# The last down product's low weight parts made by ScalarE and accumulating DMAs, its sums moved to other PSUM banks

## The chip, the cores and the metric

The kernel runs on one core of a Trainium2 chip. The metric is the device time of one execution in microseconds (us); lower is better. The number given for a kernel is the median of several executions; the profile is of one further execution.

## The reference

It is one decoder layer over 512 tokens of width 1024: a token mixer (convolution and retention branches), then a gated MLP, each followed by a residual and a LayerNorm. Only the end of the MLP matters here:

```
def channel_mixer(h, w_up, ffn_dw_w, ffn_dw_b, w_down):
    u = jnp.einsum("bsd,df->bsf", h, w_up)
    u = causal_depthwise_conv(u, ffn_dw_w, ffn_dw_b)
    val, gate = jnp.split(u, 2, axis=-1)
    return jnp.einsum("bsf,fd->bsd", val * jax.nn.silu(gate), w_down)
...
        f = channel_mixer(h, w_up[l], ffn_dw_w[l], ffn_dw_b[l], w_down[l])
        x = layer_norm(DEEPNORM_ALPHA * x + gate2 * f, ln2_g[l], ln2_b[l])
```

The einsum with w_down is (512 x 2816) by (2816 x 1024); its result is gated, added to the residual and normalised row by row.

## The kernel before

Every float32 factor is split into a high part (rounded to float32r) and a low part (the factor less its high part), and a product is made of three matmuls: high by high, low by high, high by low. In `sub_mm` these are the three `mm` lines, L1113, L1114 (both read the weight's high part) and L1115 (reads its low part).

The down product is not done as one product. Rows, columns and the sum over 2816 are each halved, and seven products of 256 x 512 outputs over 1408 (11 blocks k of 128) take the place of eight, with sums of weight blocks (T1 to T4) in place of some blocks. T1 to T4 lie in DRAM; GpSimd made them long before, with copying and accumulating DMAs (L634, L639; an accumulating DMA adds what it reads to what lies at its destination). The seventh product uses T4 = 11 blocks of 128 x 512.

Each product of the loop over n has two PSUM tiles, t = 0 and 1 (128 rows each). R1, R2 and R3 are pairs of PSUM banks that hold the sums ca, c5 and so on. Product 6 (n = 5) writes R3; the seventh, after the loop, goes on adding to R3: t = 0 over 512 columns, t = 1 over two halves of 256 columns, one after the other, so that the first half's end can be worked on while the second is multiplied. `gated` multiplies a sum by the gate row and adds it to or takes it from the residual row x; `finish` takes the LayerNorm statistics (bn_stats, bn_aggr), asks GpSimd for rstd, runs two pairs of scalar_tensor_tensor (L912, L913) on VectorE and stores two halves of 256 KB from SP's queue.

Weights come through `Stream`. For the first six products SP loads 1 MB pieces into one of two buffers (`stage`), ScalarE writes the high part `wh`, VectorE the low part `wl` = stage - wh. For the seventh, `get_into` does the same in pieces of 512 columns into pages of their own (`wph`, `wpl`), so that all 11 blocks can be there at once: 11 ScalarE instructions (L161) and 11 VectorE subtractions (L162). T4 comes in three loads, stage90 and stage91 (four blocks, 1024 KB each) and stage92 (three blocks, 768 KB); stage91's load waits for the last reader of stage89, stage92's for the last reader of stage90. The program order on each engine is set by a scheduler at build time that works with priorities; each engine then runs its rows strictly in that order.

Of the kernel before, what the change touches and what calls it, by code (L numbers as in the profile page):

```python
# [9 lines left out]
F32 = mybir.dt.float32  # L10
F32R = mybir.dt.float32r
I32 = mybir.dt.int32
AF = mybir.ActivationFunctionType
ALU = mybir.AluOpType
# [13 lines left out]
NK = NF // 2  # L28
# [74 lines left out]
class Stream:  # L103
# [44 lines left out]
            self.ready.append((wh, wl))  # L148
            self.load(i + 1)

    def get_into(self, alloc):

        nc = self.nc
        assert self.used == len(self.ready)
        i, o, w = self.subs[self.used]
        self.load(i)
        hs, ls = [], []
        for c in range(0, w, 512):
            h, l = alloc("wph", F32R), alloc("wpl", F32R)
            src = self.stage[i][:, o + c:o + c + 512]  # L160
            nc.scalar.activation(h, src, AF.Copy)  # L161
            nc.vector.tensor_tensor(l, src, h.bitcast(F32), ALU.subtract)  # L162
            hs.append(h)
            ls.append(l)
        self.load(i + 1)
        self.ready.append(None)
        self.used += 1
        return hs, ls
# [10 lines left out]
def block_kernel(ctx: ExitStack, tc: tile.TileContext, a, out):  # L179
    nc = tc.nc  # L180
    act = nc.scalar.activation
    tt = nc.vector.tensor_tensor
# [4 lines left out]
    @contextmanager  # L187
    def later(n):
        p = tc.cur_priority
        tc.cur_priority = p + n  # L190
        yield
        tc.cur_priority = p
# [8 lines left out]
    def pg(name, dt=F32, shape=(P, S)):  # L201
        uid[0] += 1
        return pgp.tile(list(shape), dt, tag="pg", bufs=NPG, name=f"{name}_{uid[0]}")

    def ps(name, shape=(P, S)):
        uid[0] += 1
        return psp.tile(list(shape), F32, tag="ps", bufs=8, name=f"{name}_{uid[0]}")
# [88 lines left out]
    st = Stream(nc, base, entries, 2)  # L296
# [20 lines left out]
    o = VEC["bada"][0]  # L317
    nc.sync.dma_start(vec[:, o:], a["vec"][:, o:])
    xh = []
    for s in range(NS):  # L320
        r = [pg("x"), pg("x")]
# [22 lines left out]
    o = VEC["bada"][0]  # L344
# [143 lines left out]
    def rotary(i, pq, e, nm):  # L488
        sw = ht("sw", [P, S])
        b = vc("bin", e)  # L490
        act(sw[0:64], pq[64:128], AF.Identity, bias=b[64:128])
        act(sw[64:128], pq[0:64], AF.Identity, bias=b[0:64])
        f = ht("t1", [P, S], bufs=2)
        stt(f, pq, b, ctab, ALU.add, ALU.mult)
        tt(sw, sw, stab, ALU.mult)
        tt(f, f, sw, ALU.add)
        xh_ = ht(nm + "h", [P, S], F32R, bufs=2 if nm == "q" else 1)
        xl_ = ht(nm + "l", [P, S], F32R, bufs=2 if nm == "q" else 1)
        split_to(xh_, xl_, f)
        return f, xh_, xl_  # L500
# [144 lines left out]
    for i in range(NH):  # L645
        if i == 0:
# [3 lines left out]
            k = rotary(i, pk, E_K + i, "k")  # L650
            v = values(i, st.get(), st.get())
        else:
# [14 lines left out]
            k = rotary(i, pk, E_K + i, "k")  # L667
# [14 lines left out]
    def gate_unit(e, j, alloc):  # L682
        p_ = ps("gate")
        fm_unit(p_, st.get(), hs)
        t = alloc("th")
        act(t, p_, AF.Tanh, bias=bhalf[:, e + j:e + j + 1], scale=0.5)
        return t
# [94 lines left out]
    def gate_row(c0, alloc, dalloc):  # L782
        rows, parts = [], []
        for half in range(2):
            dg = dalloc("dgr")
            dgh, dgl = xdg("dgh"), xdg("dgl")
            tt(dg.rearrange("p (k q) -> p k q", q=P), ident[:, None, :].broadcast_to([P, 4, P]),
               mods[:, c0 + 4 * half:c0 + 4 * half + 4].unsqueeze(2).broadcast_to([P, 4, P]), ALU.mult)
            split_to(dgh, dgl, dg)
            parts.append((dgh, dgl))  # L790
        yield None
        for half in range(2):
            dgh, dgl = parts[half]
            p_ = ps("row")
            mm(p_, onesr, dgh, start=True, stop=False)
            mm(p_, onesr, dgl, start=False, stop=True)
            r = alloc("grow")
            act(r, p_, AF.Copy)
            rows.append(r)
        yield rows  # L800
# [15 lines left out]
    for j in range(ND):  # L816
        p_ = ps("yb")
        for half in range(2):
            wh, wl = st.get()
            for kk in range(8):  # L820
                k = 8 * half + kk
# [28 lines left out]
    xs = []  # L850
# [10 lines left out]
    for j in range(ND):  # L861
        t = gate_unit(16, j, lg)
# [10 lines left out]
        x, y = pg("mh", F32R), pg("ml", F32R)  # L873
# [35 lines left out]
    def norm_rows(x, chunks, grow, brow, done=None):  # L909
        rs, nmu = layer_stats(chunks, mean_only=True)  # L910
        for j in range(2):
            stt(x[j], x[j], nmu, grow[j], ALU.subtract, ALU.mult)  # L912
            stt(x[j], x[j], rs, brow[j], ALU.mult, ALU.add)  # L913
            if done is not None:
                done(j)
# [3 lines left out]
    for half in range(2):  # L919
        wh, wl = st.get()  # L920
        for s in range(NS):
            sl = slice(s * P, (s + 1) * P)
            d = pt0[s // 2][:, s % 2]
            for kk in range(4):
                k = 4 * half + kk
                w = slice(kk * 256, (kk + 1) * 256)
                mh, ml = m_hl[k]
                f = k == 0 and s % 2 == 0
# [139 lines left out]
    for j in range(3, NF):  # L1068
        if j == 8:
            g2 = gate_row(40, cig, cig)  # L1070
# [11 lines left out]
    ca, c5, cb_, cc_ = [[dt0[:, 2 * n + t] for t in range(2)] for n in range(4)]  # L1082
    lnr = []
    for n, name in enumerate(("ln2_g", "ln2_b")):
        r = [dt1[:, 2 * n + h] for h in range(2)]
# [4 lines left out]
    g2 = rows["gate2"]  # L1090

    def finish(s, cols=(slice(0, 512),)):
        norm_rows(xs[s], [xs[s][1]] + [xs[s][0][:, c] for c in cols], ln2g, ln2b,
                  lambda j: nc.sync.dma_start(out[s * P:(s + 1) * P, j * 512:(j + 1) * 512], xs[s][j]))

    R1, R2, R3 = [[ps(f"d{n}") for _ in range(2)] for n in range(3)]


    def make(n, i):

        x, y = F[2 * i], F[2 * i + 1]
        if n == 2:
            o = split_op(i, x[:, 0:256])
            tt(x[:, 0:256], y[:, 0:256], x[:, 0:256], ALU.subtract)
            return o
        src = {3: x[:, 0:256], 4: y[:, 0:256], 5: x[:, 256:], 6: y[:, 256:]}[n]
        return split_op(i, src, neg=(n == 6))

    def sub_mm(R, o, w, c, t, d, start, stop):
        wh, wl = w  # L1110
        sl = slice(t * P, (t + 1) * P)
        r = R[t][:, d]
        mm(r, o[:, 0, sl], wh[:, c], start=start, stop=False, skip_group_check=True)  # L1113
        mm(r, o[:, 1, sl], wh[:, c], start=False, stop=False, skip_group_check=True)  # L1114
        mm(r, o[:, 0, sl], wl[:, c], start=False, stop=stop, skip_group_check=True)  # L1115

    ALL = slice(0, 512)

    def gated(x, src, g, op, dst=None):

        dst = src if dst is None else dst
        tt(dst, src, g, ALU.mult)
        tt(x, x, dst, op)

    operands = {0: ops1, 1: ops5}
    last = []
# [6 lines left out]
    for n, R in enumerate((R1, R2, R2, R2, R1, R3)):  # L1133
        new = n in (0, 1, 5)
        ops = operands.pop(n)
        made = []
        for q in range(6):
            w = st.get(ahead=min(2, 5 - q) if n == 5 else None)
            if n == 5 and q == 5:
                for _ in range(6):  # L1140
                    last += zip(*st.get_into(last_page))
            for kk in range(2 if q < 5 else 1):
                k = 2 * q + kk
                for t in range(2):
                    sub_mm(R, ops[k], w, slice(kk * 512, (kk + 1) * 512), t, ALL, new and k == 0, k == NK - 1)
                if n:
                    made.append(make(n + 1, k))
        if made:
            operands[n + 1] = made
        if n == 0:  # L1150
            for t in range(2):
                act(ca[t], R1[t], AF.Copy)
        elif n == 1:
            for t in range(2):
                act(c5[t], R2[t], AF.Copy)
        elif n == 2:
            for t in range(2):
                tt(cb_[t], R2[t], ca[t], ALU.subtract)  # L1158
            with later(60):
                for t in range(2):  # L1160
                    tt(ca[t], ca[t], g2[1], ALU.mult)
                    stt(xs[t][1], xs[t][1], ALPHA, ca[t], ALU.mult, ALU.subtract)
            with later(120):
                for t in range(2):
                    tt(c5[t], c5[t], cb_[t], ALU.subtract)
                    resid(xs[2 + t][0], c5[t], g2[0])
                    resid(xs[2 + t][1], cb_[t], g2[1])
        elif n == 3:
            for t in range(2):
                gated(xs[t][1], R2[t], g2[1], ALU.add)  # L1170
        elif n == 4:
            with later(30):
                for t in range(2):
                    resid(xs[t][0], R1[t], g2[0])
                    finish(t)
        else:
            for t in range(2):
                gated(xs[2 + t][1], R3[t], g2[1], ALU.add, cc_[t])

    ops = operands.pop(6)  # L1180
    for t, cols in ((0, (ALL,)), (1, (slice(0, 256), slice(256, 512)))):
        for c in cols:
            for k in range(NK):
                sub_mm(R3, ops[k], last[k], c, t, c, False, k == NK - 1)
            gated(xs[2 + t][0][:, c], R3[t][:, c], g2[0][:, c], ALU.subtract)
        finish(2 + t, cols)


# [95 lines left out]
```

## Time and profile before

| | |
|---|---|
| median of 3 executions | 1067.66 us (1067.57 to 1071.11) |
| profiled execution, its own time | 1068.0 us |
| its span, first to last instruction | 1066.2 us |
| TensorE (PE) busy | 1038.7 us, 97% of the span |
| VectorE (DVE) busy | 840.4 us, 79% |
| ScalarE (ACT) busy | 488.9 us, 46% |
| GpSimd (POOL) busy | 64.3 us, 6% |
| mean granted TensorE clock | 0.998 |

The time of an execution is 1.8 us more than its span. TensorE has work nearly all the time, so a change counts where it makes TensorE wait, or in what still has to run after its last matmul.

### The profile page before, as it was taken

To read this page: it belongs to the slowest core of one execution; us is meant where nothing else is said; L and a number is where in the kernel's file an instruction comes from. 1 tells how busy PE (TensorE), PEld (TensorE's weight loads), DVE (VectorE), ACT (ScalarE), POOL (GpSimd) and SP (SyncE) were. 2 spreads that over 40 slices of the span, in tenths; PEclk is the share of its full clock that TensorE was granted. 3 is DMA by queue.
4 is the path that set the end of the run, shared out by engine and by line. 5 is a ranking of instruction groups with operands and counts; after the bars stand their busy time and mean duration, and the time that the engine had idled before them with its cause. 6 is when DMAs were issued, how large, how long until landed. Compare 5 with 4: busy or idle time off the path is not lost. (4 is left out here: it accounts for less than half of the span.)

```text
span 1066.2 us, 13773 instructions
## 1 busy us (share of the span) xinstructions
PE 1038.7 (97%) x5351; PEld 883.0 (83%) x5351; DVE 840.4 (79%) x1372; ACT 488.9 (46%) x728; POOL 64.3 (6%) x77
## 2 busy tenths in 40 slices
PE   4999999999999999999999999999999999999996
PEld 2788898989898989888888888889888888887775
DVE  7989999979797979489894445777566666669897
ACT  5754444353534453461353333264444444457631
POOL 2000202020211110000000000110000000000000
PEclk9999999999999999999999999999999999999999
DMA  8822648182829392368663246112323222255562
GB/s 317 306 95 88 210 129 232 62 225 80 249 87 223 114 275 80 119 218 289 216 244 108 90 157 231 47 40 80 119 80 98 100 89 110 79 172 179 181 212 96
DMA packets 46596, 163.24 MB, mean 153 GB/s; under 512 B 4033, under 2 KB 17601, under 8 KB 35266
## 3 DMA queue, kind: packets, MB, share of 16 engines
q1 hardware_dynamic: 33922, 139.29, 37.0%
q0 software_dynamic: 12608, 23.07, 9.8%
q8 instruction: 42, 0.69, 0.2%
q14 instruction: 24, 0.20, 0.1%
HBM read 160.25 MB, written 25.17 MB: 174 GB/s over the span
## 5 line engine op out<-in xcount | busy, mean ns | idle before, releaser
L146 ACT ACTIVATE wh<-stage 128x1024 fp32r<-128x1024 f32 x177 | 185.0, 1045 | 275.0 <-PE up L467 56.1
L147 DVE TENSOR_TENSOR wl<-stage,wh 128x1024 fp32r<-128x1024 f32 x177 | 213.1, 1204 | 123.1 <-PE up L469 57.4
L485 DVE SCALAR_TENSOR_TENSOR conv<-ci,vec,conv 128x512 f32<-128x512 f32 x240 | 179.3, 748 | 2.3
L466 PE MATMUL up<-h,wh 128*128 128x512 f32 x304 | 118.3, 389 | 0.0
L467 PE MATMUL up<-h,wh 128*128 128x512 f32 x304 | 118.3, 389 | 0.0
L469 PE MATMUL up<-h,wl 128*128 128x512 f32 x304 | 75.1, 389 | 0.0
L515 PE MATMUL v<-wl,h 128*128 128x256 f32 x256 | 72.5, 283 | 0.4 <-DVE wl L147 0.4
L514 PE MATMUL v<-wh,h 128*128 128x256 f32 x256 | 72.4, 283 | 0.0
L513 PE MATMUL v<-wh,h 128*128 128x256 f32 x256 | 72.4, 283 | 0.0
L467 PEld LDWEIGHTS up<-h,wh 128*128 128x128 f32 x304 | 57.1, 188 | 11.8
L469 PEld LDWEIGHTS up<-h,wl 128*128 128x128 f32 x304 | 57.1, 188 | 11.9
L466 PEld LDWEIGHTS up<-h,wh 128*128 128x128 f32 x304 | 57.0, 188 | 11.8
L1113 PE MATMUL d<-wh,op 128*128 128x512 f32 x132 | 52.1, 396 | 0.2 <-DVE dtmp L1158 0.2
L1114 PE MATMUL d<-wh,op 128*128 128x512 f32 x132 | 52.1, 394 | 0.0
L1115 PE MATMUL d<-wl,op 128*128 128x512 f32 x132 | 51.9, 395 | 0.0
L823 PE MATMUL yb<-rh,wh 128*128 128x512 f32 x128 | 51.0, 398 | 0.0
L824 PE MATMUL yb<-rl,wh 128*128 128x512 f32 x128 | 50.5, 395 | 0.0
L825 PE MATMUL yb<-rh,wl 128*128 128x512 f32 x128 | 50.5, 395 | 0.0
L466 PE MATMUL gate<-h,wh 128*128 128x512 f32 x128 | 50.2, 392 | 0.0
L467 PE MATMUL gate<-h,wh 128*128 128x512 f32 x128 | 49.9, 390 | 0.0
L515 PEld LDWEIGHTS v<-wl,h 128*128 128x128 f32 x256 | 49.1, 192 | 0.6 <-DVE wl L147 0.6
L513 PEld LDWEIGHTS v<-wh,h 128*128 128x128 f32 x256 | 49.1, 192 | 0.0
(306 smaller groups left out, 2474.5 us busy)
## 6 DMA issues: line engine op xcount, KB each, us to landing
stage<-in_wstep SPq DMA_DIRECT2D x29, 1024.0 KB, 5.3
stage<-in_wup SPq DMA_DIRECT2D x22, 1024.0 KB, 4.8
wb<-in_wada SPq DMA_DIRECT2D x32, 512.0 KB, 5.4
stage<-in_wret SPq DMA_DIRECT2D x8, 1024.0 KB, 5.8
stage<-in_wga SPq DMA_DIRECT2D x8, 1024.0 KB, 4.8
stage<-T SPq DMA_DIRECT2D x8, 1024.0 KB, 4.9
wa<-in_wada SPq DMA_DIRECT2D x14, 512.0 KB, 7.1
T<-in_wdn POOLq DMA_DIRECT2D x4, 1024.0 KB, 13.6
```

Source lines behind the costliest of these rows:

```text
L146: nc.scalar.activation(wh[:, :w], src, AF.Copy)
L147: nc.vector.tensor_tensor(wl[:, :w], src, wh[:, :w].bitcast(F32), ALU.subtract)
L466: mm(dst, wh[:, k * P:(k + 1) * P], hs[k][0], start=(k == 0), stop=False)
L467: mm(dst, wh[:, k * P:(k + 1) * P], hs[k][1], start=False, stop=False)
L469: mm(dst, wl[:, k * P:(k + 1) * P], hs[k][0], start=False, stop=(k == n - 1))
L485: stt(o, ci[:, t:t + S], vc("cw", i * CK + t), o, ALU.mult, ALU.add)
L513: mm(d, h_h[:, k, sl], wh[:, r], start=(k == 0), stop=False)
L514: mm(d, h_l[:, k, sl], wh[:, r], start=False, stop=False)
L515: mm(d, h_h[:, k, sl], wl[:, r], start=False, stop=(k == ND - 1))
L1113: mm(r, o[:, 0, sl], wh[:, c], start=start, stop=False, skip_group_check=True)
L1114: mm(r, o[:, 1, sl], wh[:, c], start=False, stop=False, skip_group_check=True)
L1115: mm(r, o[:, 0, sl], wl[:, c], start=False, stop=stop, skip_group_check=True)
```

## The change

For the seventh product alone, `get_into` gets `adds=True`. In place of VectorE's subtraction, ScalarE writes the low part's page as minus the high part, and a DMA issued by GpSimd adds the weight block to it out of DRAM (T4), 256 KB each: 11 VectorE instructions go, 11 ScalarE instructions and 11 accumulating DMAs come. Each low part has to wait for its ScalarE instruction and then for its DMA.

The seventh product no longer adds to R3. It starts fresh sums: t = 0 in R1[0], t = 1 in R2[0] (columns 0 to 255) and R2[1] (256 to 511). R3, the sum of product 6, is put into x by four further VectorE instructions (a multiplication and a subtraction for each t) ahead of it.

```diff
-    def get_into(self, alloc):
+    def get_into(self, alloc, adds=False):
...
             nc.scalar.activation(h, src, AF.Copy)
-            nc.vector.tensor_tensor(l, src, h.bitcast(F32), ALU.subtract)
+            if adds:
+                nc.scalar.activation(l, h.bitcast(F32), AF.Copy, scale=-1.0)
+                for f, x in self.entries[i][0]:
+                    nc.gpsimd.dma_start(l[:, f], x[:, (o + c) // 512], accum_op=ALU.add)
+            else:
+                nc.vector.tensor_tensor(l, src, h.bitcast(F32), ALU.subtract)
...
-                    last += zip(*st.get_into(last_page))
+                    last += zip(*st.get_into(last_page, adds=True))
...
+    for t in range(2):
+        tt(c5[t], R3[t], g2[0], ALU.mult)
+        tt(xs[2 + t][0], xs[2 + t][0], c5[t], ALU.subtract)
     ops = operands.pop(6)
-    for t, cols in ((0, (ALL,)), (1, (slice(0, 256), slice(256, 512)))):
-        for c in cols:
+    H = (slice(0, 256), slice(256, 512))
+    for t, parts in ((0, [(R1[0], ALL, ALL)]), (1, [(R2[h], H[0], H[h]) for h in range(2)])):
+        for r, d, c in parts:
             for k in range(NK):
-                sub_mm(R3, ops[k], last[k], c, t, c, False, k == NK - 1)
-            gated(xs[2 + t][0][:, c], R3[t][:, c], g2[0][:, c], ALU.subtract)
-        finish(2 + t, cols)
+                sub_mm({t: r}, ops[k], last[k], c, t, d, k == 0, k == NK - 1)
+            gated(xs[2 + t][0][:, c], r[:, d], g2[0][:, c], ALU.subtract)
+        finish(2 + t, [c for _, _, c in parts])
```

In the rows below, d2_838 and d2_839 are R3[0] and R3[1], d0_834 is R1[0], d1_836 and d1_837 are R2[0] and R2[1]; wph_896 to wph_916 are the high parts of blocks 0 to 10 (even numbers), wpl_897 to wpl_917 the low parts. What stands in brackets is what a row waits for: an engine, or a DMA (DMASW: one issued by GpSimd, DMAHW: one issued by SP). In the rows of the changed kernel the line numbers are 6 higher than before.

TensorE at the start of the seventh product, before:

```order
L1113 MATMUL d2_838_8294<-wph_896_9090,op_886_8992 128x512 [waits DVE_49,Activation_49]
L1114 MATMUL d2_838_8294<-wph_896_9090,op_886_8992 128x512
L1115 MATMUL d2_838_8294<-wpl_897_9091,op_886_8992 128x512
L1113 MATMUL d2_838_8294<-wph_898_9094,op_887_9001 128x512 [waits Activation_49]
L1114 MATMUL d2_838_8294<-wph_898_9094,op_887_9001 128x512
L1115 MATMUL d2_838_8294<-wpl_899_9095,op_887_9001 128x512
```

and with the change:

```order
L1119 MATMUL d0_834_8290<-wph_896_9090,op_886_8992 128x512 [waits Activation_49]
L1120 MATMUL d0_834_8290<-wph_896_9090,op_886_8992 128x512
L1121 MATMUL d0_834_8290<-wpl_897_9091,op_886_8992 128x512 [waits DMASW4_49]
L1119 MATMUL d0_834_8290<-wph_898_9095,op_887_9001 128x512 [waits Activation_49]
L1120 MATMUL d0_834_8290<-wph_898_9095,op_887_9001 128x512
L1121 MATMUL d0_834_8290<-wpl_899_9096,op_887_9001 128x512 [waits DMASW5_49]
L1119 MATMUL d0_834_8290<-wph_900_9102,op_888_9014 128x512 [waits Activation_49]
L1120 MATMUL d0_834_8290<-wph_900_9102,op_888_9014 128x512
```

The first row no longer waits for VectorE; each row that reads a low part now waits for a DMA of GpSimd.

TensorE at the end of the seventh product, from the row that waits for block 9's low part (wpl_915) on, with the change:

```order
L1121 MATMUL d0_834_8290<-wpl_915_9140,op_895_9087 128x512 [waits DMASW6_49]
L1119 MATMUL d0_834_8290<-wph_916_9144,op_918_9155 128x512
L1120 MATMUL d0_834_8290<-wph_916_9144,op_918_9155 128x512 [waits DVE_49]
L1121 MATMUL d0_834_8290<-wpl_917_9145,op_918_9155 128x512 [waits DMASW4_49]
L1119 MATMUL d1_836_8292<-wph_914_9139,op_895_9087 128x256
L1120 MATMUL d1_836_8292<-wph_914_9139,op_895_9087 128x256
L1121 MATMUL d1_836_8292<-wpl_915_9140,op_895_9087 128x256
L1119 MATMUL d1_836_8292<-wph_916_9144,op_918_9155 128x256
L1120 MATMUL d1_836_8292<-wph_916_9144,op_918_9155 128x256
L1121 MATMUL d1_836_8292<-wpl_917_9145,op_918_9155 128x256
L1120 MATMUL d1_837_8293<-wph_908_9124,op_892_9060 128x256
L1121 MATMUL d1_837_8293<-wpl_909_9125,op_892_9060 128x256
```

Behind the wait for wpl_915 stand three more rows of d0, six of d1_836 and fourteen of d1_837, of which the first two are shown. Before, 33 rows of 256 columns, the whole second half of t = 1, stood last.

VectorE at the end, before, from the multiplication of the first half of t = 1 on (mv_78, rstd_80, xr_628 and xr_629 belong to t = 0, mv_81, xr_635 and xr_636 to t = 1):

```order
L1122 TENSOR_TENSOR d2_839_8295<-d2_839_8295,grow_758_7297 128x256 [waits PE_49]
L243 BN_AGGR mv_78_9189<-bnst_918_9186 128x2 [waits DVE_49]
L1123 TENSOR_TENSOR xr_635_5884<-xr_635_5884,d2_839_8295 128x256 [waits DVE_49]
L245 TENSOR_SCALAR ve_79_9191<-mv_78_9189 128x1 [waits DVE_49]
L912 SCALAR_TENSOR_TENSOR xr_628_5812<-xr_628_5812,mv_78_9189,drow_8285 128x512
L912 SCALAR_TENSOR_TENSOR xr_629_5814<-xr_629_5814,mv_78_9189,drow_8285 128x512
L913 SCALAR_TENSOR_TENSOR xr_628_5812<-xr_628_5812,rstd_80_9193,drow_8285 128x512 [waits DVE_49,Pool_49]
L913 SCALAR_TENSOR_TENSOR xr_629_5814<-xr_629_5814,rstd_80_9193,drow_8285 128x512 [waits DVE_49]
L241 BN_STATS bnst_919_9271<-xr_635_5884 128x6
L1122 TENSOR_TENSOR d2_839_8295<-d2_839_8295,grow_758_7297 128x256 [waits PE_49]
L1123 TENSOR_TENSOR xr_635_5884<-xr_635_5884,d2_839_8295 128x256 [waits DVE_49]
```

and with the change, from the same step on:

```order
L1129 TENSOR_TENSOR xr_635_5884<-xr_635_5884,d1_836_8292 128x256 [waits DVE_49]
L247 BN_STATS bnst_918_9201<-xr_628_5812 128x6 [waits DVE_49]
L1128 TENSOR_TENSOR d1_837_8293<-d1_837_8293,grow_758_7297 128x256 [waits PE_49]
L249 BN_AGGR mv_78_9204<-bnst_918_9201 128x2 [waits DVE_49]
L247 BN_STATS bnst_919_9286<-xr_635_5884 128x6
L251 TENSOR_SCALAR ve_79_9206<-mv_78_9204 128x1 [waits DVE_49]
L918 SCALAR_TENSOR_TENSOR xr_628_5812<-xr_628_5812,mv_78_9204,drow_8285 128x512
L918 SCALAR_TENSOR_TENSOR xr_629_5814<-xr_629_5814,mv_78_9204,drow_8285 128x512
L919 SCALAR_TENSOR_TENSOR xr_628_5812<-xr_628_5812,rstd_80_9208,drow_8285 128x512 [waits DVE_49,Pool_49]
L919 SCALAR_TENSOR_TENSOR xr_629_5814<-xr_629_5814,rstd_80_9208,drow_8285 128x512 [waits DVE_49]
L1129 TENSOR_TENSOR xr_635_5884<-xr_635_5884,d1_837_8293 128x256
L247 BN_STATS bnst_919_9286<-xr_635_5884 128x6 [waits DVE_49]
```

The multiplication of the second half of t = 1 stood behind the whole LayerNorm of t = 0 (mv_78 to the two rstd_80 rows); now it stands ahead of it.

## Rows read from the trace of the kernel before

**Rows 1.** Windows: us, busy of PE, PEld, DVE, ACT, POOL, PEclk, DMA share, GB/s

```profile
1039.50:1041.20 1.70, 0.04 (x1) 0.01 (x1) 1.70 (x5) 0.33 (x1) 0.00 (x0) 1.00 0.96 378
1041.20:1058.40 17.20, 15.99 (x99) 14.23 (x99) 14.31 (x27) 3.54 (x7) 0.89 (x1) 1.00 0.24 82
```

**Rows 2.** Timeline of PE: start us, us, instruction, [idle before, releaser]

```profile
1039.14 0.40 PE L1115 MATMUL d<-wl,op 128*128 128x512 f32 x1
1041.22 0.47 PE L1113 MATMUL d<-wph,op 128*128 128x512 f32 x1 [1.68 <-DVE dtmp L1122]
...
1058.05 0.28 PE L1115 MATMUL d<-wpl,op 128*128 128x256 f32 x1
```

**Rows 3.** Chain that ended last: start us, us, what, in the seventh product

```profile
1049.93 0.23 PE d L1114
...
1057.97 0.12 PE d L1113
```

**Rows 4.** Timeline of DVE while PE waited

```profile
1039.78 0.69 DVE L162 TENSOR_TENSOR wpl<-stage,wph 128x512 fp32r<-128x512 f32 x1
1040.38 0.69 DVE L1122 TENSOR_TENSOR dtmp<-d,grow 128x512 f32<-128x512 f32 x1
```

**Rows 5.** Timeline of ACT: the high parts of T4's first two loads

```profile
1033.96 2.20 ACT L161 ACTIVATE wph<-stage 128x512 fp32r<-128x512 f32 x4 [0.96 <-DMA stage<-T]
1040.87 2.19 ACT L161 ACTIVATE wph<-stage 128x512 fp32r<-128x512 f32 x4 [4.71 <-DMA stage<-T]
```

**Rows 6.** Timeline of SP, and stage91's DMA: KB, us to landing

```profile
1035.84 0.33 SPq L130 DMA_DIRECT2D stage<-T  x1
1038.29 0.99 SPq L1094 DMA_DIRECT2D out<-xr  x2
...
stage<-T SPq DMA_DIRECT2D x1, 1024.0 KB, 5.0
```

**Rows 7.** Timeline of POOL, accumulating DMAs at 316 us; the first one's landing

```profile
316.64 1.34 POOL L639 DMA_DIRECT2D T<-in_wdn  x1
317.48 1.80 POOL L639 DMA_DIRECT2D T<-in_wdq  x1
...
T<-in_wdn POOLq DMA_DIRECT2D x1, 512.0 KB, 6.2
```

**Rows 8.** DMA queues (packets, MB, share) in 388.5:394.5, 330:340 (two), 1029.4:1034

```profile
q0 software_dynamic: 620, 1.24, 112.3%
...
q0 software_dynamic: 1447, 1.42, 89.4%
q1 hardware_dynamic: 176, 1.10, 27.9%
...
q1 hardware_dynamic: 144, 1.05, 67.5%
```

**Rows 9.** Timeline of DVE in the last 13 us

```profile
1053.51 0.20 DVE L243 BATCH_NORM_AGGREGATE mv<-bnst 128x2 f32<-128x12 f32 x1
1053.64 0.42 DVE L1123 TENSOR_TENSOR xr<-xr,d 128x256 f32<-128x256 f32 x1
...
1054.04 1.40 DVE L912 SCALAR_TENSOR_TENSOR xr<-xr,mv,drow 128x512 f32<-128x512 f32 x2
1055.36 1.41 DVE L913 SCALAR_TENSOR_TENSOR xr<-xr,rstd,drow 128x512 f32<-128x512 f32 x2
1056.68 0.42 DVE L241 BATCH_NORM_STATS2 bnst<-xr 128x6 f32<-128x256 f32 x1
1058.37 0.43 DVE L1122 TENSOR_TENSOR d<-d,grow 128x256 f32<-128x256 f32 x1 [1.26 <-PE d L1115]
...
1061.42 1.41 DVE L913 SCALAR_TENSOR_TENSOR xr<-xr,rstd,drow 128x512 f32<-128x512 f32 x2
```

**Rows 10.** Windows behind the last matmul, columns as in rows 1

```profile
1061.00:1062.00 1.00, 0.00 (x0) 0.00 (x0) 1.00 (x2) 0.00 (x0) 0.24 (x1) 1.00 0.00 0
...
1063.00:1064.00 1.00, 0.00 (x0) 0.00 (x0) 0.00 (x0) 0.00 (x0) 0.00 (x0) 0.50 1.00 371
```

## The prediction

> **What bounds the kernel now.** I read the page's shares first: TensorE is busy 97% of the span, so the change can only act where TensorE waits, or behind its last matmul. It touches nothing ahead of the seventh product, so I then read windows and TensorE's timeline there. TensorE stops once for 1.68 us before the product's first matmul [rows 2], with VectorE busy for the whole of that window [rows 1]. The timeline names the releaser: the multiplication L1122 that empties product 6's bank began only at 1040.38, behind low parts of weights (L162) that stand ahead of it in VectorE's queue [rows 4]. From 1041.22 the product runs to 1058.33 (the last matmul starts at 1058.05 and takes 0.28) [rows 2] at a pitch of 0.23 us for 512 columns and 0.12 for 256 [rows 3]; 33 and 66 matmuls are 33 x 0.23 + 66 x 0.12 = 15.5 us of work. The DMA engines have little to do meanwhile, 24% of that window [rows 1]. Last, VectorE's timeline: it starts on the last sum at 1058.37 and ends its last instruction at 1061.42 + 1.41 = 1062.83 [rows 9]; the stores end the span at 1066.2.
>
> **The change, part by part.**
>
> *The start.* The seventh product writes R1[0], which is free by then, so its first matmul need not wait for VectorE. It can start where the matmuls before it end their turn, 1039.14 + 0.23 = 1039.4 in place of 1041.2. That is a gain of up to 1.8 us, if nothing else is late. VectorE loses 11 subtractions and gets four instructions of 512 columns; it is not waited for there any more, so both are costed at nothing. The cover is the wait for DMAs, next; without it, the four would cost 4 x 0.6 = 2.4 us (pitch from 1039.78 to 1040.38 [rows 4]) only if the fresh sums were done before 1045, and they are not.
>
> *ScalarE.* It begins on T4's first load at 1033.96, and four instructions take 2.20 us, a pitch of 0.53 and some 0.62 for one alone [rows 5]. Now high and low parts alternate, and a low part reads the high part just made. I take 0.67 between those two (the whole 0.62 and a little), so the first low part stands at 1033.96 + 0.67 + 0.62 = 1035.3, and GpSimd can issue the first DMA. Stage91 needs 4 high and 4 low parts, stage92 3 and 3: 14 instructions, some 8.1 us from the landing of stage91.
>
> *The accumulating DMAs.* This is the term that decides. No accumulating DMA into on-chip memory is in the trace; the nearest are those that GpSimd made into DRAM. Alone, one of 512 KB landed 6.2 us after its issue, and issues follow at 317.48 - 316.64 = 0.84 us [rows 7]. In a stretch where only they ran, the engines were full (share 112%, overlapping packets) and moved 1.24 MB in 6 us, 206 GB/s. A load by SP moved 1.05 MB in 67.5% of 4.6 us, 338 GB/s. The two add up: where both ran, 1.42 MB / 206 + 1.10 MB / 338 = 6.9 + 3.3 = 10.2 us of work was done in 10 us [rows 8]. So accumulating costs 1.64 times a plain load per byte, and both queues share the same engines.
>
> Now the work from about 1037 on. Eleven blocks of 128 x 512 x 4 bytes are 2.88 MB: 14.0 us at 206. Stage91 is issued at 1035.84 as before [rows 6], 1.05 MB or 3.1 us; stage92 (0.79 MB) takes 2.3 us; the pair of stores at 1038.29 [rows 6] (0.52 MB) 1.5 us. Together 20.9 us. The first DMA is issued at 1035.3; of its 6.2 - 2.5 = 3.7 us that are not transfer I put 2.1 ahead of the data and 1.6 behind, so from 1037 there is always something to move if ScalarE keeps ahead. It does: stage91, 5.0 us to landing when alone [rows 6], now shares the engines and lands near 1043, and 1043 + 8.1 = 1051 is eight microseconds ahead of the end of the transfers at 1037 + 20.9 = 1057.9. GpSimd's issues, 11 x 0.84, lie inside that too. The last DMA lands at 1057.9 + 1.6 = 1059.5. Lower bound of the price: the load's rate, 338, and 8.5 us in place of 14.0. Upper bound: nothing faster than the rows, and the clock (below). I take 206, since the addition has to read both operands wherever they lie, and the rows show that this costs engine time and not only latency.
>
> The Trainium skill would have it cheaper: "DMA: Bandwidth & Descriptors", section "Anatomy of one DMA — SWDGE (gpsimd) path", gives 2.0 us plus bytes / 436e3 for a DMA issued by GpSimd, which is 2.6 us (an estimate) for 256 KB. By that the transfers would be out of the way and the time would be that of the first rival below. For 512 KB the same line gives 3.2 us where the trace has 6.2, so I do not follow it for an accumulating DMA.
>
> *TensorE.* Its rows stand in the order shown, and each row that reads a low part waits for its DMA. It starts at 1039.4, then waits for block after block; what it has in hand it works off between landings. Behind the landing of the last one (wpl_915) it still has 4 matmuls of 512 and 6 + 14 of 256: 4 x 0.23 + 20 x 0.12 = 3.3 us. So VectorE can take the last sum at 1059.5 + 3.3 + 0.1 = 1062.9, against 1058.37: **+4.5 us**.
>
> *Behind the last matmul.* Before, the LayerNorm of t = 0 was done while TensorE multiplied the second half of t = 1: the aggregation at 1053.51 took 0.13 until the next row, the four scalar_tensor_tensor ran from 1054.04 to 1056.68, and bn_stats of the first half followed [rows 9]. Now the multiplication that waits for TensorE's last sum stands ahead of these in VectorE's queue, as the order shows. So they run behind it: 0.13 + 2.64 + about 0.3 for bn_stats, **+3.1 us** ahead of the last subtraction. Nothing hides it, since only t = 1's own statistics are left behind it.
>
> *Sum.* 1068.0 (the profiled execution) + 4.5 + 3.1 = 1075.6. That execution is 0.3 us above the median of the runs, so I predict **1075.3 us**, 0.7% above 1067.66. About 0.5%, 5.3 us, is what a measurement of this kernel can tell from no change: the borders are 1062.3 and 1073.0.
>
> **The rivals.**
>
> *Accumulating is as cheap as loading (ends on the other side: no change).* At 338 GB/s the engines would have 8.5 + 6.9 = 15.4 us of work and finish at 1052.4, and ScalarE would be last: stage91 near 1042, + 8.1 = 1050.1, + 3.7 + 0.8 for the DMA = 1054.6. Then VectorE starts at 1058.0, 0.4 earlier than before, and the sum is -0.4 + 3.1 = +2.7: 1070.4. For it: the destination is on chip and need not be read from DRAM. Against it: the share of the engines in [rows 8]. It decides at 11.7 us of accumulating in place of 14.0, that is 246 GB/s; above that the result is within 0.5%.
>
> *No landing is ever late.* Then the product ends at 1039.4 + 15.5 = 1054.9, 3.4 us earlier, and 3.1 of that goes to the moved LayerNorm: 1067.4. It would need the last block on chip by 1052, before ScalarE has even written its minus part if stage91 lands at 1043. This is also the floor: nothing in the change makes the kernel more than 0.5% faster.
>
> *The clock falls.* The granted clock was 1.00, the level of 2.4 GHz, through the 1.7 us stop [rows 1] and still at 1061 to 1062; it stood at 0.50, 1.2 GHz, only at 1063, almost 5 us after the last matmul [rows 10]. With the change TensorE waits several times from 1039.4 on, with 0.69 us of work for each of the first blocks, and a fall is possible. If the last 3.3 us ran at 1.2 GHz they would take 6.6: 1078.6. The Trainium skill, "TensorE: Matmul & The Clock Gate", section "Part 1: The HAM clock gate", says that an engine gone idle is put to 1.2 GHz until it is busy again; the trace's tail agrees with the fall and shows no return.
>
> **How the numbers follow.** My forecast (1072 to 1077.5) gets 0.50, with the clock 0.15, cheap accumulating 0.30, no late landing 0.03, something else 0.02. Most of the forecast lies above 1073.0, a little under it goes to "same": slower 0.65, same 0.33, faster 0.02. The range reaches from the lower edge of the cheap case to past the case of the clock: 1069.5 to 1079.5; the forecast's own is 1072 to 1077.5.
>
> **What would show it.** The first matmul of the seventh product starts at 1039.4 and waits for no VectorE row; the low parts wait for DMAs, with several microseconds of TensorE idle in all; the queue of GpSimd's DMAs shows 2.88 MB more at a share that gives about 206 GB/s, and the engines are full from 1037 to 1058; stage91 lands later than 5 us; the last multiplication begins near 1063, and both LayerNorms stand behind it. The prediction is wrong if the accumulating DMAs land at the pace of ScalarE, about 1.2 us a block from 1039 on, or if TensorE stops for something that I have not named.

## The result and the profile after

The changed kernel takes 1078.8 us (median of 6 runs, 1078.08 to 1079.88) where the kernel before takes 1067.84 beside it: ratio 1.010, 95% interval 1.0089 to 1.011. The profiled execution took 1078.99 us, its span is 1077.2. Against the forecast of 1075.3 that is slower still: inside the range (1069.5 to 1079.5), near its upper end, and 1.3 us above the forecast's own 1072 to 1077.5.

TensorE's timeline around and in the seventh product (of 100 rows, those with a wait and the ends):

```profile
1040.03 0.39 PE L1121 MATMUL d<-wl,op 128*128 128x512 f32 x1
1040.26 0.39 PE L1119 MATMUL d<-wph,op 128*128 128x512 f32 x1
...
1043.99 0.80 PE L1121 MATMUL d<-wpl,op 128*128 128x512 f32 x1 [3.11 <-DMA wpl<-T]
...
1045.98 0.80 PE L1121 MATMUL d<-wpl,op 128*128 128x512 f32 x1 [0.34 <-DMA wpl<-T]
...
1047.98 0.79 PE L1121 MATMUL d<-wpl,op 128*128 128x512 f32 x1 [0.35 <-DMA wpl<-T]
...
1050.97 0.50 PE L1121 MATMUL d<-wpl,op 128*128 128x512 f32 x1 [1.13 <-DMA wpl<-T]
...
1061.15 0.50 PE L1121 MATMUL d<-wpl,op 128*128 128x512 f32 x1 [1.20 <-DMA wpl<-T]
...
1062.40 0.50 PE L1121 MATMUL d<-wpl,op 128*128 128x512 f32 x1 [0.17 <-DMA wpl<-T]
...
1065.69 0.28 PE L1121 MATMUL d<-wpl,op 128*128 128x256 f32 x1
```

Set beside [rows 2]: the sixth product's last matmul starts at 1040.03, not 1039.14. This 0.89 us came up ahead of everything that the change touches; in the profiled executions below the same row lies anywhere from 1038.70 to 1040.41, on both sides of 1039.14. The stop in front of the product is gone. In its place TensorE stands six times, 6.3 us, always for a low part that a DMA has not landed: for those of the first four blocks, and ten microseconds later for two of the last.

Windows of the same stretch. The columns are those of [rows 1]: the third figure from the right is the granted clock, the next the busy share of the DMA engines, the last GB/s:

```profile
1036.00:1038.00 2.00, 2.00 (x10) 1.60 (x10) 2.00 (x7) 1.97 (x4) 1.32 (x2) 1.00 0.86 248
...
1042.00:1044.00 2.00, 0.01 (x1) 0.01 (x1) 2.00 (x4) 1.24 (x3) 0.00 (x0) 0.76 1.09 213
1044.00:1046.00 2.00, 1.66 (x4) 0.84 (x4) 2.00 (x4) 1.94 (x5) 1.36 (x2) 0.50 1.11 262
...
1050.00:1052.00 2.00, 1.03 (x5) 0.90 (x6) 0.00 (x0) 0.62 (x2) 0.00 (x0) 1.00 1.10 227
...
1056.00:1058.00 2.00, 2.00 (x16) 1.87 (x15) 0.00 (x0) 0.00 (x0) 0.51 (x1) 1.00 0.98 138
```

The clock fell to 0.50 (1.2 GHz) after TensorE had stood from 1040.9 on, and was back at 1.00 (2.4 GHz) from 1050. The DMA engines are full or nearly so from 1036 to 1060 (shares of 0.81 to 1.12), but "full" goes with 138 GB/s in one window and 262 in another.

The DMA view of 1035 to 1069 (queues: packets, MB, share of the 34 us; issues: KB each, median us to landing):

```profile
q0 software_dynamic: 1584, 2.88, 49.4%
q1 hardware_dynamic: 864, 2.88, 26.0%
...
wpl<-T POOLq DMA_DIRECT2D x11, 256.0 KB, 7.7
...
stage<-T SPq DMA_DIRECT2D x1, 1024.0 KB, 6.0
stage<-T SPq DMA_DIRECT2D x1, 768.0 KB, 11.1
```

The packets of GpSimd's queue took 0.494 x 34 = 16.8 us for 2.88 MB, 171 GB/s. Packets overlap (the share passes 1 in three of the windows shown), so this packet time is not time on the clock. The load of 768 KB is stage92 (three blocks): 11.1 us to landing.

ScalarE's timeline (stage91's blocks, then stage92's), and GpSimd's behind it:

```profile
1042.73 0.63 ACT L162 ACTIVATE wph<-stage 128x512 fp32r<-128x512 f32 x1 [2.80 <-DMA stage<-T]
...
1046.29 0.61 ACT L162 ACTIVATE wph<-stage 128x512 fp32r<-128x512 f32 x1
1051.38 0.63 ACT L162 ACTIVATE wph<-stage 128x512 fp32r<-128x512 f32 x1 [4.48 <-DMA stage<-T]
1051.92 0.61 ACT L164 ACTIVATE wpl<-wph 128x512 fp32r<-128x512 f32 x1
```

```profile
1047.15 0.86 POOL L166 DMA_DIRECT2D wpl<-T  x1 [0.79 <-ACT wph L162]
1052.83 0.86 POOL L166 DMA_DIRECT2D wpl<-T  x1 [4.83 <-ACT wpl L164]
1053.87 2.63 POOL L166 DMA_DIRECT2D wpl<-T  x3 [0.18 <-issue]
```

ScalarE stands 4.48 us for stage92, and GpSimd, with nothing to issue, 4.83 us; the last four DMAs go out from 1052.83 on. By the count of rows one of these four is of stage91: its low part, at 1051.92, stands in ScalarE's queue behind the first high part of stage92, though ScalarE was free from 1046.90 on. That another order would have gained time was not tried.

The time to landing of the DMAs issued at 1047.15, 1052.83 and 1053.87 (the DMA view of a window round each issue):

```profile
wpl<-T POOLq DMA_DIRECT2D x1, 256.0 KB, 7.9
...
wpl<-T POOLq DMA_DIRECT2D x1, 256.0 KB, 4.3
...
wpl<-T POOLq DMA_DIRECT2D x1, 256.0 KB, 5.9
```

So the seventh of the eleven landed at 1055.0, the eighth at 1057.1, the ninth at 1059.8.

VectorE's tail, which answers to [rows 9]:

```profile
1063.62 1.15 DVE L1128 TENSOR_TENSOR d<-d,grow 128x512 f32<-128x512 f32 x2 [17.48 <-PE d L1121]
...
1066.20 0.41 DVE L1128 TENSOR_TENSOR d<-d,grow 128x256 f32<-128x256 f32 x1
...
1066.98 1.40 DVE L918 SCALAR_TENSOR_TENSOR xr<-xr,mv,drow 128x512 f32<-128x512 f32 x2
...
1072.20 1.41 DVE L919 SCALAR_TENSOR_TENSOR xr<-xr,rstd,drow 128x512 f32<-128x512 f32 x2
```

The last sum is taken at 1066.20 in place of 1058.37, +7.83, of which 0.89 is the shift from upstream; VectorE then works 7.41 us to its end (1073.61) where it worked 4.46, +2.95. The stores add 0.2. That is the whole difference of the two spans, 11.0 us. The chain that ended last, its longest steps from 1036 on (start, length):

```profile
1036.72 5.99 DMA stage<-T
...
1048.01 4.81 issue
...
1055.58 6.78 DMA wpl<-T
```

The last accumulating DMA was issued at 1055.58 and landed 6.78 us later, at 1062.36: the wait that ends at 1062.40 above.

### The profile page after: what moved, and what is told of

It is laid out like the page before. It is cut to its first block, busy times and chain, and to the rows that moved or that the text cites. A ratio compares the mean times of both kernels' runs of the same rounds, so it can differ in the third digit from the quotient of the medians.

```text
span 1077.2 us, 13804 instructions
## 1 busy us (share of the span) xinstructions
PE 1042.5 (97%) x5351; PEld 884.1 (82%) x5351; DVE 835.5 (78%) x1365; ACT 495.5 (46%) x739; POOL 72.8 (7%) x88
## 5 line engine op out<-in xcount | busy, mean ns | idle before, releaser
L146 ACT ACTIVATE wh<-stage 128x1024 fp32r<-128x1024 f32 x177 | 185.1, 1046 | 279.9 <-PE up L473 56.1
```

What stands on the lines that cost most here:

```text
L146: nc.scalar.activation(wh[:, :w], src, AF.Copy)
```

## The experiments

The theory after this profile: the new banks cost nothing, and the loss is all from the accumulating DMAs, by late landings in two places (the first four blocks and the last ones), with the clock's fall as a consequence. The rivals: the order of VectorE's queue takes 3.1 us of it, as the prediction had it; ScalarE's second instruction; the bytes alone; the clock as the main cause. All edits are to the changed kernel.

**The banks alone** (`banks_only`): low parts by VectorE's subtraction.

```diff
-                    last += zip(*st.get_into(last_page, adds=True))
+                    last += zip(*st.get_into(last_page))
```

> The new PSUM banks with VectorE's subtraction as before; no accumulating DMA. My theory (the late low parts cost the time, the banks cost none): TensorE starts the seventh product near 1039.5 of its span without the 1.7 us stop, ends its 15.5 us of work near 1055.5, and the LayerNorm of t = 0 comes behind the last sum, about 3 us; the two cancel: 1066 to 1068.5 us. Rival (the banks, or the rows' new order on TensorE and VectorE, carry a good part of the loss): 1071 us or more.

Measured 1067.8 us (11 runs), ratio 0.9988 (0.998 to 0.9997). TensorE doesn't wait once in the seventh product, and VectorE takes the last sum at 1054.66:

```profile
1051.31 1.03 DVE L1128 TENSOR_TENSOR d<-d,grow 128x512 f32<-128x512 f32 x2 [0.18 <-PE d L1121]
...
1054.66 0.43 DVE L1128 TENSOR_TENSOR d<-d,grow 128x256 f32<-128x256 f32 x1
...
1060.48 1.41 DVE L919 SCALAR_TENSOR_TENSOR xr<-xr,rstd,drow 128x512 f32<-128x512 f32 x2
```

The last sum is taken 3.7 us earlier than in [rows 9], yet VectorE ends only 0.9 us earlier (1061.89 against 1062.83), since from 1051.31 on it is itself without a gap; 0.4 us of both is a shift from upstream (the sixth product's last matmul starts at 1038.74). By the ratio this half of the change is worth 0.12%, 1.3 us, with an interval from 0.3 to 2.1: far less than the 0.5% that the prediction names as what a measurement can tell, though two further runs below with the new banks and no DMAs give the same.

**The DMAs alone** (`adds_only`): sums in R3 as before, low parts as in the change (the product's code is that of the kernel before).

> ScalarE's minus part and the accumulating DMAs, with the sums in R3 as before. My theory: the last landing is as late as in the changed kernel, near 1062.4 of the span; behind it TensorE has 4 x 0.23 + 5 x 0.12 + 33 x 0.12 us and a stop of 1.1 for the bank, so the last sum comes near 1069.3, with 4.5 us of VectorE and 3.4 of stores behind it: a span of 1077, a time of 1077.5 to 1080.5. Rival (the banks carry part of the loss): under 1075 us.

Measured 1079.11 us, ratio 1.0093 (1.0079 to 1.0107): the whole loss. TensorE waits 6.0 us for the DMAs in five places, of which 0.51 us is for one of the last blocks.

**The last multiplication pinned behind t = 0's LayerNorm** (`after_pin`), the order of VectorE's queue, to which the prediction put 3.1 us:

```diff
+                with tc.issue_after(ends[-1].ins):
+                    gated(xs[2 + t][0][:, c], r[:, d], g2[0][:, c], ALU.subtract)
```

> The changed kernel with the last multiplication pinned behind the LayerNorm of t = 0 in VectorE's queue. The step of the prediction (the order of VectorE's queue costs 3.1 us): about 1075.7 us. Rival, read from the trace of the changed kernel (VectorE works without a gap from 1063.62 to its end, because the sum of t = 0 itself comes only 2.6 us ahead of the last one): the queue's order gives back 0.3 us at most, 1078.3 to 1079 us.

Measured 1079.15 us, ratio 1.0093: no gain. The multiplication of the last sum moved to 1069.74, and the LayerNorm ran ahead of it, but it had to wait for its own sum, the first of these rows:

```profile
1063.88 1.15 DVE L1130 TENSOR_TENSOR d<-d,grow 128x512 f32<-128x512 f32 x2 [16.91 <-PE d L1123]
...
1069.74 0.42 DVE L1130 TENSOR_TENSOR d<-d,grow 128x256 f32<-128x256 f32 x1
```

This profile shows one thing more. TensorE stands four times, 5.6 us, for the first four blocks, the last time at 1051.30, and not at all for the last ones (its waits, in all, times and longest, and a window, below): the clock stood at 0.50 up to 1054, later than in the changed kernel, and by the time that TensorE came to the last blocks they had landed. The product takes 25.7 us from its first matmul to its end, the same 25.7 as in the changed kernel.

```profile
PE d L1123 <- DMA wpl<-T: 5.6, 4, 3.1
...
1052.00:1054.00 2.00, 2.00 (x9) 1.81 (x8) 0.00 (x0) 2.00 (x4) 0.60 (x1) 0.50 1.12 204
```

The same pin on the banks alone (`banks_pin`) changes nothing either:

> The new banks with VectorE's subtraction, and the last multiplication pinned behind the LayerNorm of t = 0. In the run without the pin VectorE worked without a gap from 1051.31 to its end, so the order can give back only some 0.4 us (a multiplication of 256 columns that no longer stands ahead): 1067 to 1068 us. If the order cost 3 us after all: 1065 us or less.

Measured 1067.73 us, ratio 0.9988 (0.998 to 0.9997), the same as without it.

**ScalarE's part without the DMAs** (`no_dma`):

```diff
-                for f, x in self.entries[i][0]:
-                    nc.gpsimd.dma_start(l[:, f], x[:, (o + c) // 512], accum_op=ALU.add)
```

> The change without its eleven accumulating DMAs; the low parts stay at minus the high parts, so the addition of the original weights is left out. ScalarE's 22 instructions, the new banks and everything else stand. Theory A (the whole loss comes from the transfers: late low parts, and stage92 late beside them): stage92 lands in 4 to 5 us again, TensorE stops for less than 1 us in the seventh product, the granted clock stays at 1.00, the last sum is taken between 1054.5 and 1056.5, and the time is 1067.0 to 1069.0 us. Theory B (ScalarE's second instruction for each block is a good part of it: the high parts of stage91 and stage92 come 2 to 3 us later, since each waits behind a low part): TensorE waits for ScalarE for 2 us or more, and the time is 1069.5 to 1072 us.

Measured 1067.28 us, ratio 0.9989 (0.998 to 0.9999). TensorE's matmuls show no wait in the seventh product, though stage92 took 6.3 us and not 4 to 5. The product takes 16.8 us where the banks alone took 15.7, but the time is no longer. So ScalarE's eleven more instructions cost nothing in the end, and the loss lies in the transfers.

**Copies in place of additions** (`plain_copy`): `accum_op` left out of the call, so that the low parts are the original weights; same bytes, same queue.

> The 11 DMAs copy instead of accumulating (the low parts are then the whole weights: this part of the computation is changed). Same count, bytes, issues and waits. My theory (the engine time of accumulating is what is late, and it delays the load of stage92 too): copies at about 338 GB/s take 8.5 us in place of 14, stage92 lands near 1047 in place of 1051, the last low part lands near 1056, the span ends near 1070.5: 1071 to 1074 us. Rival (count, issue and latency of the 11 DMAs, or the chain through ScalarE, are what is late): 1077 us or more.

Measured 1074.47 us, ratio 1.0055 (1.0041 to 1.0069). The DMA view of 1035 to 1063:

```profile
q0 software_dynamic: 1584, 2.88, 37.2%
...
wpl<-T POOLq DMA_DIRECT2D x11, 256.0 KB, 4.9
...
stage<-T SPq DMA_DIRECT2D x1, 768.0 KB, 9.0
```

The packets of the copies take 0.372 x 28 = 10.4 us for the 2.88 MB (276 GB/s), those of the additions 16.8 (171): 1.6 times as much per byte. Adding in place of copying accounts for about half of the loss; the other half is left even with copies, since TensorE still waits 2.25 us for the first low part (at 1042.00), 3.4 in all, and the clock falls to 0.50 behind it (1044 to 1046).

**Half the columns** (`half_bytes`): each DMA adds 256 of the 512 columns, the rest stays minus the high part.

```diff
-                    nc.gpsimd.dma_start(l[:, f], x[:, (o + c) // 512], accum_op=ALU.add)
+                    nc.gpsimd.dma_start(l[:, 0:256], x[:, (o + c) // 512, 0:256], accum_op=ALU.add)
```

> All 11 accumulations, each over 256 of its 512 columns (the other half of the low parts stays minus the high part: this part of the computation is left out). Same issues, waits and ScalarE rows, half of the bytes: 7 us of accumulating instead of 14, a little less engine time than the plain copies had. If engine time is what is late, 1072 to 1075 us, like the plain copies; if it is the count and the latency of the DMAs, 1077 us or more.

Measured 1075.1 us, ratio 1.0062 (1.0048 to 1.0076), a little above what was expected.

```profile
q0 software_dynamic: 1584, 1.44, 35.0%
...
wpl<-T POOLq DMA_DIRECT2D x11, 128.0 KB, 5.2
...
stage<-T SPq DMA_DIRECT2D x1, 768.0 KB, 8.2
```

Half the bytes in the same number of packets take 9.8 us of packet time, 0.58 of the whole, and the landing falls only from 7.7 to 5.2. TensorE still stands 4.7 us for the first four blocks.

**Only blocks 0 to 3, and only the last three, by DMA** (`first_four`, `last_three`); VectorE subtracts for the others:

```diff
-                for _ in range(6):
-                    last += zip(*st.get_into(last_page, adds=True))
+                for i in range(6):
+                    last += zip(*st.get_into(last_page, adds=i < 2))     # last_three: adds=i >= 4
```

> Only the first four blocks' low parts come by ScalarE and accumulating DMAs; the other seven by VectorE, as before. Theory A (the prediction's: the end of all transfers sets the time): with 4 instead of 11 accumulations, 5 us of them instead of 14, nothing is in flight near the end, and the time is 1068 to 1071 us. Theory B (read from the changed kernel's trace: TensorE takes the blocks in order, stood until the fourth low part at 1050.97, and had 12.4 us of work left there, so that the last sum could not come before 1063.4): the late first four alone keep most of the loss, 1073 to 1076.5 us.

> Only the last three blocks' low parts come by ScalarE and accumulating DMAs. Stage92 lands near 1047 as before, ScalarE's six instructions end near 1051, three accumulations (3.9 us) and a latency of 3.7 bring the last landing to 1055.5 or so, with 3.3 us of TensorE behind it: theory A gives 1070 to 1073 us. Theory B (the first blocks carry the loss): 1067.5 to 1070 us.

The first four: 1076.66 us, ratio 1.0067 (1.0052 to 1.0083), just above theory B. The last three: 1075.18, ratio 1.0059 (1.0045 to 1.0073), a miss for both theories, which had at most 1073. TensorE's one wait in the product with the last three, the windows behind it, and the DMA view:

```profile
1055.81 0.50 PE L1121 MATMUL d<-wpl,op 128*128 128x512 f32 x1 [3.72 <-DMA wpl<-T]
```

```profile
1056.00:1058.00 2.00, 2.00 (x7) 1.70 (x7) 0.00 (x0) 0.00 (x0) 0.00 (x0) 0.58 0.10 16
1058.00:1060.00 2.00, 2.00 (x9) 1.71 (x9) 0.70 (x1) 0.00 (x0) 0.00 (x0) 0.56 0.00 0
```

```profile
stage<-T SPq DMA_DIRECT2D x1, 768.0 KB, 4.3
wpl<-T POOLq DMA_DIRECT2D x3, 256.0 KB, 5.6
```

With no load beside them three additions still take 5.6 us to land (the first, issued at 1049.50 with nothing ahead of it, 4.3), and they begin when ScalarE has stage92. What I had left out was the clock: it stood at 0.58 and 0.56 in the two windows of 2 us behind this wait, which is some 1.7 us of full-rate work lost, most of the miss. The first four alone cost 8.1 us and the last three 6.6, where all eleven cost 11, so the two don't add up: what TensorE loses early it makes good in part while it would stand for the last blocks anyway.

**What the half clock costs** (`four_filled`): the kernel of the first four, with 21 further matmuls into a bank that is read no more, where TensorE stood.

```diff
+        for _ in range(fill):
+            mm(R1[1], o[:, 0, sl], wh[:, c], start=True, stop=True, skip_group_check=True)
         mm(r, o[:, 0, sl], wl[:, c], start=False, stop=stop, skip_group_check=True)
...
+                       (12, 2, 2, 5)[k] if t == 0 and k < 4 else 0)
```

> The kernel with only blocks 0 to 3 by DMA (1076.66 us, granted clock 0.50 from 1043 to 1056, last matmul at 1066.42), with 12, 2, 2 and 5 further matmuls of 512 columns into a bank that is read no more, each group just ahead of the low part's matmul of blocks 0 to 3 that TensorE waits for there; 21 x 0.23 = 4.8 us of work where it stood 5.4 us. Theory A (standing lowers the clock, and the half rate costs time behind the fourth landing): the granted clock stays at 1.00, the fourth low part's matmul still starts near 1051.1, since its DMA sets it, and the product ends 13.0 us later (0.23 + 21 x 0.23 + 66 x 0.12) in place of 15.6: last sum taken near 1064.5, time 1073 to 1075 us. Theory B (the rate of 0.43 us a matmul has another cause, such as the transfers beside it, or costs nothing since landings set the pace to the end): the clock or the pitch stays low, or the time is 1076 us or more, with the further matmuls on top of it.

Measured 1074.23 us, ratio 1.0055 (1.004 to 1.007). Since the two kernels stood beside different runs of before, both ran again together:

> Once more the kernel with only blocks 0 to 3 by DMA, on one chip with the filled one, since the two stood beside different runs of the kernel before (ratios 1.0067 and 1.0055, their intervals overlap) while the profiles show 2.9 us between them from the product's first matmul to the last sum (27.4 and 24.5 us). Theory A (the half clock costs 2 to 3 us): a ratio between 1.006 and 1.008. Theory B (the filled kernel gained nothing and the two calls differ by their chips): both ratios within 0.001 of each other.

> The filled kernel again, beside the unfilled one. Theory A: 2 to 3 us below it, a ratio between 1.004 and 1.0055. Theory B: within 1 us of it.

Measured 1076.46 us, ratio 1.0068 (1.0055 to 1.0082), and 1074.01 us, ratio 1.0047 (1.0035 to 1.006): 2.4 us less with more work. Windows of the first profile of each, unfilled and then filled:

```profile
1052.00:1054.00 2.00, 2.00 (x6) 1.54 (x5) 2.00 (x4) 0.87 (x2) 0.00 (x0) 0.50 0.00 0
1054.00:1056.00 2.00, 2.00 (x8) 1.71 (x8) 1.56 (x3) 0.00 (x0) 0.00 (x0) 0.50 0.00 0
1056.00:1058.00 2.00, 2.00 (x13) 1.88 (x12) 0.00 (x0) 0.00 (x0) 0.00 (x0) 0.84 0.00 0
```

```profile
1044.00:1046.00 2.00, 1.34 (x6) 0.86 (x5) 1.90 (x4) 1.63 (x4) 0.00 (x0) 1.00 1.10 259
...
1052.00:1054.00 2.00, 2.00 (x9) 1.67 (x10) 1.27 (x3) 1.68 (x3) 0.00 (x0) 1.00 0.00 0
```

Unfilled, TensorE is busy all through 1052 to 1056 with no DMA beside it, and at half clock; filled, the clock never leaves 1.00. In the second pair the fourth low part's matmul starts at 1050.52 unfilled and 1050.37 filled: up to there landings set the pace and the clock costs nothing. All of the 2.4 us is made behind it.

## Why the prediction was right, and where its sum was short

*The start.* Right: the product's first matmul follows the one before without a wait, at 1040.26; less the shift of 0.89 that is 1.85 us earlier than 1041.22, 1.8 predicted. The fresh banks also take away a second stop, which the sum contains (15.5 us of work in 17.1) but the prediction doesn't name: before, the second half of t = 1 waited 1.12 us for VectorE to be done with the bank. The banks alone show what both are worth at the end of the kernel.

```profile
1054.11 0.39 PE L1113 MATMUL d<-wph,op 128*128 128x256 f32 x1 [1.12 <-DVE ve L245]
```

*ScalarE.* Its paces were right (0.65 and 0.54 between rows, 0.67 and 0.53 taken), and stage91 landed at 1042.7, less the shift 1041.8, 1043 predicted. "ScalarE keeps ahead" was wrong: the prediction costed stage92 by its bytes and nothing for its latency beside the additions. It took 11.1 us to land, so ScalarE stood 4.48 us for it and GpSimd could issue the last four DMAs only from 1052.83 on, where 1051 had been the end of all.

*The accumulating DMAs, the term that decides.* The mechanism stands, and the price per byte fits; the supply fell short. The fifth to the seventh addition, issued at 1044.32, 1045.50 and 1047.15, landed 8.1, 8.2 and 7.9 us later, so 1.3 us apart, where 206 GB/s gives 1.27. At the prediction's prices seven additions, both loads and the pair of stores are 8.9 + 3.1 + 2.3 + 1.5 = 15.8 us, so the seventh would land at 1037 + 15.8 + 1.6 = 1054.4; it landed at 1055.0, less the shift 1054.1. Only the last four came late: 1062.4, less the shift 1061.5, against 1059.5. They took 7.3 us behind the seventh and not 4 x 1.27 = 5.1, since the first of them was issued only at 1052.83 and landed 4.3 us later; an addition with nothing ahead of it takes as long (`last_three`). So the step that fell is "there is always something to move": 0.8 us of the delay lies ahead of the eighth landing, 1.4 between the eighth and the ninth, which the late issues alone don't explain. The 171 GB/s of packet time is no proof of a lower rate: by packet time [rows 8] give 1.24 MB in 1.123 x 6 = 6.7 us, 184 GB/s, where the prediction's 206 is bytes by the clock. Its 338 for a load goes by packet time, so its 1.64 mixes the two measures, and the 1.6 between additions and copies, both in packet time, doesn't confirm it. The Trainium skill's line in "DMA: Bandwidth & Descriptors", section "Anatomy of one DMA — SWDGE (gpsimd) path", from which I estimated 2.6 us for 256 KB, is below every landing here: 2.9 us for a copy with hardly anything beside it (`plain_copy`, issued at 1049.66) and 4.9 in the median of the eleven, 4.3 for an addition with nothing ahead of it, 5.6 in the median of three, 7.7 of eleven.

*TensorE.* That it would stand between landings and work off 3.3 us behind the last one: 3.6 measured (1062.40 to 1065.97). So +4.5 became +6.9 (7.83 less the shift), 2.0 of the 2.4 by the later landing. But the prediction priced only the last landing. The early stops, with the clock that falls behind them, are a second path of about the same length: the first four blocks alone kept 8.1 us of the loss, and the pinned kernel reached the same time without standing for the last blocks at all. Which of the two ends last differs between profiles of much the same time (1.4 us of standing at the end here, 0.5 in `adds_only`, none in `after_pin`), so that the predicted path alone comes near the measured time is in part luck.

*Behind the last matmul.* +3.1 predicted, +2.95 measured, for a reason that fell: the order of VectorE's queue was said to cost it. Turned round by the pin, it gained nothing, so the agreement of the two sizes is luck. With the last weights late, t = 0's own sum is taken at 1063.62, 2.6 us ahead of t = 1's last, and VectorE has no gap from there on: whichever comes first, both LayerNorms lie behind the late landing. A late weight delays both halves, since each block is used by both.

*The rivals.* Cheap accumulating (1070.4) was to decide from 246 GB/s up; copies moved 276 by packet time and still gave 1074.47, since not the rate but the first landings were late by then. No late landing (1067.4, "the floor"): the banks alone, 1067.8, and the run without the DMAs, 1067.28, are this case, and nothing was faster by 0.5%. The falling clock gave 1078.6, close to the result, but not in its way: it was to fall in the last 3.3 us, and these ran at 1.00. It fell after the first stop instead. By the rows at 1061.15 and 1062.40 it costs nothing at the end of this profile, since TensorE stands again for the last landings; in the pinned kernel's it lasts longer and takes up that standing; where no landing is late behind it, it costs 2.4 us, as the filled kernel showed. The profile after shows what the tail of before could not [rows 10]: the return to 1.00, in the window from 1050, once TensorE had been busy most of the time from 1044 on. That is as the Trainium skill has it in "TensorE: Matmul & The Clock Gate", section "Part 1: The HAM clock gate".

Not settled: of the 7.7 us, 4.3 are what an addition takes with nothing ahead of it; how the other 3.4 divide between the additions ahead and the loads beside isn't shown, nor is the 1.4 us between the eighth landing and the ninth. A third buffer for the staged weights, which might have taken stage92 out of the DMAs' way, wasn't tried.

## What to carry to other kernels

A transfer that takes a cheap subtraction's place must be costed by its time to landing beside all other transfers that are then under way, and so must these others: the load behind it can be the first to be late. A wait of the engine that bounds the kernel can cost more than its length, since the matmuls behind it may run at half rate; work thrown away in the gap gave part of that back. When two edits come together, time each alone: here one was worth some 1.3 us (0.3 to 2.1), which could not be seen beside the ten that the other cost.

## What the runs showed that I had not expected

The busy share of the DMA engines is no measure of their rate: at shares of 0.98 to 1.11 they moved 138 to 262 GB/s in the windows shown. A load of 768 KB by SP took 11.1 us to land beside additions, 9.0 beside copies, 6.3 beside only another load and stores (`no_dma`), 4.3 with none of them beside it (`last_three`). GpSimd needed 0.86 us to issue each addition. The stop of 1.68 us before [rows 1, 2] left the clock at 1.00; the one of 3.1 us here did not, and with three more short ones behind it the clock was back only in the window from 1050.
